# Eight Strassen pairs in each feed-forward layer, the first of them begun in the first token half

## The chip, the cores and the metric

The kernel runs on one core of a Trainium2 chip. The metric is the time of one execution on the device in microseconds (us), less is better. Two kernels are compared by the median of several runs on the same chip.

## The reference

Two layers over one sequence of 512 tokens with 1024 channels. Layer 0 mixes the tokens with a causal multi-scale pooling, layer 1 with a causal differential attention; a SwiGLU feed-forward part follows each. All is fp32.

```python
D_MODEL, SEQ, DEPTH = 1024, 512, 2
D_FF = 2816

def _swiglu(x, w_gate, w_up, w_down):
    return (jax.nn.silu(x @ w_gate) * (x @ w_up)) @ w_down

def reference(x, ...):
    for i in range(DEPTH):
        h = _multiscale_pool(...) if i % 2 == 0 else _diff_attention(...)
        x = _layernorm(ALPHA * x + h, ln_mix_g[i], ln_mix_b[i])
        x = _layernorm(ALPHA * x + _swiglu(x, w_gate[i], w_up[i], w_down[i]), ln_ffn_g[i], ln_ffn_b[i])
    return x
```

## The kernel before

**Numbers in two halves.** Each fp32 factor is split into a high and a low part of a shorter type. A product is three matmuls, high by high, high by low and low by high. A weight chunk of 512 KB comes from HBM into a tile `raw` (five of them), ACT casts its high part (`h`), and DVE subtracts to get the low part (`l`). Six pairs of weight tiles exist; a cast into one of them must wait until the product that last used it has ended. The tokens lie transposed in `xt`, in two halves of 256.

**Gate and up.** The 2816 hidden features are 22 blocks of 128, each with a gate and an up product. They are computed in three ways, in this order:
- *Early features*: while the mixer's last token blocks (2 and 3) are still being normalised and transposed, only the first token half exists. Layer 0 takes three features, layer 1 two, at 256 tokens, and then the same features once more for the second half. The dictionary `late` says after which product of the first half PE transposes block 2 or 3.
- *Plain features*: full width, 512 tokens, 48 matmuls of 512 for gate and up.
- *Strassen pairs*, `strassen(k)`: two features by two token halves make a 2x2 block product, done with seven half-size products of 24 matmuls of 256 instead of eight. The order on PE is `GATE = ("P1", "Q5", "P6", "Q3", "P7", "P2", "Q4")`. P1, P6, P7 and Q4 accumulate in the PSUM bank A, Q5 and Q3 in C, P2 in B. After a product the bank's content is read, by ACT or DVE, before the next product in that bank adds to it. Before, pairs 4 to 10 are done this way, seven in each layer.

P1 and P2 multiply token half 0 by plain weight chunks. The other products need sums: sums of weight chunks, which DVE adds in the raw tiles (line 636), and sums of the tokens' quarters, which DVE and ACT make once per layer (`sums_of_x`, lines 690 to 714, with their low parts in `xs`, line 696). DVE also makes the gated product `hid` (line 677), the layer norm's affine pair on the residual (227, 228), the sums of the down weights' terms (750, 751) and the sums of finished hidden rows (`sum_hidden`, 776 to 783). In a pair DVE subtracts Q3 (line 921) and P7 (line 923) from their banks.

**What sets the order.** The program is scheduled by hand: each engine executes its instructions in the order in which the code issues them. `advance` and `ahead` issue the steps that ready weight chunks, six chunks ahead of PE, in the order of the list `steps`. `ready` does that for the first chunks of a layer, `fetch` issues the loads on SP. `catch_up` issues one step of each open generator in `behind`. In the head of layer 0, `summed(s, ...)` (lines 183 and 190) adds the mixer's output to the residual of token block s and takes its statistics, `spread_of` ends them with a power on POOL (199), and `norm` (208) scales.

Of the kernel before, what the change touches and what calls it, by code (L numbers as in the profile page):

```python
# [12 lines left out]
F32 = mybir.dt.float32  # L13
# [3 lines left out]
ALU = mybir.AluOpType  # L17
# [37 lines left out]
def trunk(ctx, tc, x, wall, pscale, lam_p, subln, table, lng, lnb, band, first, onehot, out):  # L55
# [6 lines left out]
    def bank(name):  # L62
        return ps.tile([P, 512], F32, tag="bank", name=name)
# [19 lines left out]
    def load_x(s):  # L83
# [8 lines left out]
    divided = [0]  # L92
    total = wall.shape[0]
# [8 lines left out]
    rows_of_wall = list(range(total))  # L102
    rows_of_wall[attn : attn + 24] = order_of_rows
    added = {attn + 6 + r: vrow[1] + r for r in range(2)}
# [206 lines left out]
    with tc.tile_pool(name="pool", bufs=1) as pp:  # L311
# [221 lines left out]
    def ffn(layer, late):  # L533
        n = 2 * layer + 1
        final = n == 2 * DEPTH - 1
        c0 = base[0]
        c1 = c0 + 2 * FB
        tt = nc.vector.tensor_tensor
        with tc.tile_pool(name=f"ffn{layer}", bufs=1) as fp:
# [12 lines left out]
            def block(i, b):  # L552

                if PAIRS[i][1] == 2:
                    return wall[c1 + 4 * i + b]
                return wall[c1 + 20 + b // 2][:, (b % 2) * 512 : (b % 2 + 1) * 512]

# [31 lines left out]

            chunks, index, steps = [], {}, []  # L590

# [5 lines left out]

            for k in range(HALF):
                j0 = index[k] = len(chunks)
                c = c0 + 4 * k  # L600
                if k in SPLIT:

                    chunks += [(c, ()), (c, (c, c + 1)), (c, (c, c + 2)), (c + 2, ())]
                    chunks += [(c + 1, (c + 1, c + 2)), (c + 3, ()), (c, (c, c + 3))]
                    step("cast", j0)
                    for w in (
                        "low 0, sum 1, cast 1, sum 4, cast 3, cast 4, low 1, sum 2, cast 2, low 3, "
                        "low 2, sum 6, cast 5, cast 6, low 4, low 5, low 6"
                    ).split(", "):
                        steps.append((w[:-2], j0 + int(w[-1])))  # L610
                else:
                    for i in range(4):
                        chunks.append((c + i, ()))
                        step("cast", j0 + i)
                        step("low", j0 + i)
            uses = {}
# [114 lines left out]
            def load_terms(k):  # L731
                if k < HALF - 1:
                    c = c1 + 4 * (k // 2)
                    src = wall[c : c + 4][:, :, term_slice(k)].rearrange("(j r) p t -> p j r t", j=2)
                else:
                    src = wall[c1 + 20 : c1 + 22].rearrange("j p (r t) -> p j r t", r=2)
# [33 lines left out]
            def sum_hidden(k):  # L770
# [3 lines left out]
                u = fp.tile([P, 2, 256], F32, tag="u", name=f"u{layer}_{k}", bufs=1)  # L774
                v = fp.tile([P, 2, 2, 256], F32R, tag="v", name=f"v{layer}_{k}", bufs=2)
                tt(u[:, 0, :], first, second, op=ALU.subtract)
# [54 lines left out]
            sums = sums_of_x()  # L831
            ks = [range(4 * b, 4 * b + 4) for b in range(2)]
            by_part = [(0, 0, range(KB)), (0, 1, range(KB)), (1, 0, range(KB))]
            by_half = [(0, 0, ks[0]), (1, 0, ks[0]), (0, 0, ks[1]), (1, 0, ks[1])]
            by_half += [(0, 1, ks[1]), (0, 1, ks[0])]
            for lo in (0, 256):
                for f in range(early):
                    for i in range(2):
                        product(
                            accs[f][i], 2 * f + i, lo, lo + 256,  # L840
                            None if layer or lo else by_part if f or i else by_half,
                        )
                        if not lo and (f, i) in late:
                            late[f, i]()
                        if not lo:
                            advance(2 * early, True)
                    if lo:
                        advance(2 * f + 6)
# [3 lines left out]
                        if f < 2:  # L852
                            weight_sums()
                            next(sums)
                        if f == 1:
                            behind.append(sum_hidden(0))

            def plain(f):
                k = f // 2
                j = index[k] + 2 * (f % 2)  # L860
                a = (bank(f"g{layer}_{f}"), bank(f"u{layer}_{f}"))
# [7 lines left out]
                if f < SB:  # L869
                    affine(n - 1, f)  # L870
                if f in (3, 5, 7):
                    weight_sums()
# [5 lines left out]
            def strassen(k):  # L878
                names = {"P1": "A", "P6": "A", "P7": "A", "Q4": "A", "Q5": "C", "Q3": "C", "P2": "B"}
                banks = {b: bank(f"{b}{layer}_{k}") for b in "ACB"}  # L880
                lefts = {
                    "P1": [quarter(0, i, 0) for i in range(2)],
                    "P2": [quarter(0, i, 1) for i in range(2)],
                    "Q4": [quarter(1, i, 1) for i in range(2)],
                }
                for m, p in enumerate(("Q5", "P6", "P7", "Q3")):
                    lefts[p] = [xs[:, m, i] for i in range(2)]
# [3 lines left out]
                def both(t):  # L891
                    return t.rearrange("p (f t) -> p f t", f=2)
# [4 lines left out]
                for j, p in enumerate(GATE):  # L897
                    acc = banks[names[p]]
                    h, l = halves[index[k] + j]
                    xh, xl = lefts[p]  # L900
                    for f in range(2):
                        o = acc[:, f * 256 : (f + 1) * 256]
                        for kk in range(4):
                            c = slice((4 * f + kk) * P, (4 * f + kk + 1) * P)
                            for e, (w, x) in enumerate(((h, xh), (h, xl), (l, xh))):
                                nc.tensor.matmul(  # L906
                                    o, w[:, c], x[:, kk, :],
                                    start=p in ("P1", "Q5", "P2") and f + kk + e == 0,
                                    stop=p in ("Q4", "Q3", "P2") and (f, kk, e) == (1, 3, 2),
                                    skip_group_check=True,  # L910
                                )
                    acc = both(acc)
# [16 lines left out]
                    ahead(index[k] + j + 6)  # L929
                    catch_up()  # L930
# [116 lines left out]
    def attention():  # L1047
        n = 2
        with tc.tile_pool(name="attn", bufs=1) as ap:
# [420 lines left out]

    ffn(0, {(1, 0): later(0, 2), (1, 1): later(0, 3)})
    attention()
# [109 lines left out]
```

## Time and profile before

| | |
|---|---|
| median of three runs | 939.98 us (939.54 to 940.16) |
| the profiled execution | 940.01 us, span 938.2 us |
| mean granted clock of PE | 0.998 |
| PE busy | 925.0 us, 99% |
| DVE busy | 789.8 us, 84% |
| ACT busy | 512.9 us, 55% |
| POOL busy | 126.7 us, 14% |
| mean DMA rate | 225 GB/s |

The time of an execution is 1.8 us longer than the span from the first to the last instruction. PE's share of the span leaves 13.2 us in which it had no matmul. A row of a timeline gives start, duration, engine, line, operation, output and inputs, the shape, the count, and in brackets the idle time ahead of it with what ended that. Lines are those of the kernel before.

### The profile page before, as it was taken

To read this page: it belongs to the slowest core of one execution; us is meant where nothing else is said; L and a number is where in the kernel's file an instruction comes from. 1 tells how busy PE (TensorE), PEld (TensorE's weight loads), DVE (VectorE), ACT (ScalarE), POOL (GpSimd) and SP (SyncE) were. 2 spreads that over 40 slices of the span, in tenths; PEclk is the share of its full clock that TensorE was granted. 3 is DMA by queue.
4 is the path that set the end of the run, shared out by engine and by line. 5 is a ranking of instruction groups with operands and counts; after the bars stand their busy time and mean duration, and the time that the engine had idled before them with its cause. 6 is when DMAs were issued, how large, how long until landed. Compare 5 with 4: busy or idle time off the path is not lost.

```text
span 938.2 us, 14939 instructions
## 1 busy us (share of the span) xinstructions
PE 925.0 (99%) x5710; PEld 827.2 (88%) x5710; DVE 789.8 (84%) x1166; ACT 512.9 (55%) x814; POOL 126.7 (14%) x152
## 2 busy tenths in 40 slices
PE   9999999999999999999999999999999999999996
PEld 8998899999988888888888887988899999988884
DVE  8969889999988778968888877788789999987678
ACT  6652444555564457667878754734245554654450
POOL 4221121110101201201112100211111110001101
PEclk9999999999999999999999999999999999999999
DMA  8487988886868988975666522597887885878942
GB/s 243 154 266 225 336 283 245 259 258 211 259 199 277 363 256 232 226 198 154 164 137 178 159 68 68 148 322 226 258 255 243 266 277 192 264 244 286 353 156 91
DMA packets 86038, 211.11 MB, mean 225 GB/s; under 512 B 15140, under 2 KB 26660, under 8 KB 85966
## 3 DMA queue, kind: packets, MB, share of 16 engines
q1 hardware_dynamic: 43420, 117.16, 38.1%
q0 software_dynamic: 18768, 58.20, 24.8%
q10 hardware_dynamic: 23778, 34.78, 10.4%
q8 instruction: 45, 0.74, 0.3%
q14 instruction: 27, 0.22, 0.1%
HBM read 173.40 MB, written 36.72 MB: 224 GB/s over the span
## 4 chain that ended last, share of the span: by engine, by line
PE 92%; DVE 5%; ACT 1%; issue 1%; DMA 0%; POOL 0%; DVEq 0%; ACTq 0%; POOLq 0%
PE A L906 17%; PE P L973 14%; PE C L906 9%; PE Q L973 6%; PE B L906 4%; PE g L150 3%; PE u L150 3%; PE g L149 3%; PE u L151 3%; PE u L149 3%; PE g L151 3%; PE s L1192 2%; PE va L1123 2%; PE wo L150 1%; PE wo L151 1%; PE q L149 1%
## 5 line engine op out<-in xcount | busy, mean ns | idle before, releaser
L636 DVE TENSOR_TENSOR raw<-raw,raw 128x1024 f32<-128x1024 f32 x56 | 68.3, 1219 | 0.5
L123 ACT CAST xs<-hid 128x512 fp32r<-128x512 f32 (+1 forms) x60 | 34.7, 581 | 24.4 <-DVE hid L813 24.4
L124 DVE TENSOR_TENSOR xs<-hid,xs 128x512 fp32r<-128x512 f32 (+1 forms) x60 | 38.5, 643 | 7.8 <-ACT xs L123 7.8
L1212 ACT ACTIVATE p<-p,mn 128x128 f32<-128x128 f32 (+3 forms) x64 | 35.2, 552 | 14.1 <-DVE mn L1207 14.1
L249 ACT ACTIVATE y<-pt,bT,gT 128x128 f32<-128x128 f32 x72 | 27.1, 456 | 26.6 <-PE pt L235 23.5
L744 POOL DMA_DIRECT2D b<-in_wall x20 | 14.0, 706 | 172.4 <-DMA tsum<-b 68.8
L805 POOL DMA_DIRECT2D xs<-ssum x24 | 17.4, 725 | 140.8 <-PE Q L973 67.8
L677 DVE TENSOR_TENSOR hid<-sg,u 128x512 f32<-128x512 f32 x16 | 11.0, 687 | 25.5 <-PE u L151 14.7
L199 POOL TENSOR_TENSOR rs<-rs,mhalf 128x1 f32<-128x1 f32 x16 | 12.8, 800 | 140.9 <-DVE rs L198 97.3
L744 POOL DMA_DIRECT2D hid<-in_wall x24 | 18.9, 831 | 77.5 <-DMA tsum<-hid 50.2
L1207 DVE CUSTOM_DVE_ANT_0 p<-s,bias 128x128 f32<-128x128 f32 (+3 forms) x64 | 28.0, 485 | 1.1 <-PE s L1192 1.1
L781 ACT CAST v<-u 128x512 fp32r<-128x512 f32 x22 | 13.7, 621 | 26.9 <-DVE u L779 26.8
L190 DVE BATCH_NORM_STATS2 st<-res 128x6 f32<-128x512 f32 x32 | 22.2, 694 | 1.1
L932 ACT ACTIVATE sg<-sg 128x512 f32<-128x512 f32 x14 | 8.9, 633 | 26.0 <-DVE sg L925 26.0
L745 POOL DMA_DIRECT2D hid<-in_wall x12 | 14.8, 1233 | 55.1 <-DMA hid<-in_wall 55.1
L693 ACT CAST xs<-hid 128x1024 fp32r<-128x1024 f32 x8 | 8.4, 1051 | 24.0 <-DVE hid L710 11.6
L124 DVE TENSOR_TENSOR xt<-y,xt 128x512 fp32r<-128x512 f32 x18 | 12.3, 691 | 10.9 <-ACT xt L123 10.7
L921 DVE TENSOR_TENSOR hid<-C,hid 128x512 f32<-128x512 f32 x14 | 9.7, 691 | 10.7 <-PE C L906 9.2
L1226 DVE SCALAR_TENSOR_TENSOR p<-p,sm,p 128x128 f32<-128x128 f32 (+3 forms) x32 | 17.6, 551 | 1.1
L917 ACT COPY hid<-C 128x512 f32<-128x512 f32 x14 | 8.2, 588 | 18.2 <-PE C L906 18.2
L124 POOL TENSOR_TENSOR sql<-sq,sqh 128x512 fp32r<-128x512 f32 x7 | 9.3, 1324 | 60.5 <-ACT sqh L123 60.5
L745 POOL DMA_DIRECT2D b<-in_wall x10 | 12.3, 1230 | 38.0 <-DMA b<-in_wall 38.0
(1211 smaller groups left out, 3637.1 us busy)
## 6 DMA issues: line engine op xcount, KB each, us to landing
raw<-in_wall SPq DMA_DIRECT2D x122, 512.0 KB, 5.0
r<-tsum SPq DMA_DIRECT2D x40, 512.0 KB, 4.5
hid<-in_wall POOLq DMA_DIRECT2D x36, 512.0 KB, 7.3
b<-in_wall POOLq DMA_DIRECT2D x30, 512.0 KB, 5.8
r<-in_wall SPq DMA_DIRECT2D x30, 512.0 KB, 4.5
tsum<-hid ACTq DMA_DIRECT2D x24, 512.0 KB, 5.4
ssum<-v ACTq DMA_DIRECT2D x22, 512.0 KB, 3.8
tsum<-b ACTq DMA_DIRECT2D x20, 512.0 KB, 4.9
```

The costliest lines, as they stand in the source:

```text
L123: nc.scalar.copy(dst_h, src)
L124: (low or nc.vector).tensor_tensor(dst_l, src, dst_h.bitcast(F32), op=ALU.subtract)
L149: nc.tensor.matmul(acc, ah, bh, start=start, stop=False)
L150: nc.tensor.matmul(acc, ah, bl, start=False, stop=False)
L151: nc.tensor.matmul(acc, al, bh, start=False, stop=stop)
L249: nc.scalar.activation(y[:, k, :], pt[:, k * P : (k + 1) * P], AF.Identity, bias=bT[:, n, kk : kk + 1], scale=gT[:, n, kk : kk + 1],)
L636: tt(t, raws[pair[0]], raws[pair[1]], op=ALU.add)
L744: nc.gpsimd.dma_start(out=t[:, j], in_=src[:, j])
L906: nc.tensor.matmul(o, w[:, c], x[:, kk, :], start=p in ("P1", "Q5", "P2") and f + kk + e == 0, stop=p in ("Q4", "Q3", "P2") and (f, kk, e) ...
L973: nc.tensor.matmul(accs[s], x[:, k, r], y[:, c], start=first and k == 0 and e == 0, stop=last and k == m - 1 and e == 2, skip_group_check= ...
L1207: nc.vector.tensor_tensor_reduce(out=p, in0=accs[c], in1=biases[h][:, w - 1 :: -1] if w < S else biases[h][:, ::-1], op0=ALU.add, op1=ALU. ...
L1212: nc.scalar.activation(p, p, AF.Exp, bias=mn[:, q, c : c + 1], scale=-1.0, accum_out=sm[:, q, c : c + 1],)
```

## The change

The number of Strassen pairs goes from seven to eight in each layer: pair 3 is a pair now. Layer 0 has two early features instead of three and four plain ones instead of five, layer 1 one instead of two and five instead of six. In the place of the early feature that went, the first token half has P1 and P2 of pair 3, whose two weight chunks are fetched there, and fetched again when pair 3's other products come (four more loads of 512 KB in all). Their sum waits in a tile `g3` of its own. `strassen(3)` skips P1 and P2.

Other edits come with it. In layer 0 the transposes of token block 3 stand behind P1 instead of behind the up product of feature 1. The weight chunk of that up product (`w5`) is made ready ahead of `summed(3)`. The first product of the second token half goes by half of the channels. The tile `v` has one buffer instead of two. The first two steps of `sums_of_x` come in the first half. At the end of the attention the second of two scalings comes behind `ready` instead of ahead of it. DVE has 1169 rows instead of 1149, PE 4433 instead of 4472 (a row may stand for several instructions), SP 240 instead of 236.

```diff
-SPLIT = (4, 5, 6, 7, 8, 9, 10)
+SPLIT = (3, 4, 5, 6, 7, 8, 9, 10)
+EARLY = (2, 1)
...
+    def rows_of_ffn(layer, c):
+        g = list(range(c, c + 2 * FB))
+        e, pair = 2 * EARLY[layer], c + 4 * SPLIT[0]
+        return g[:e] + [pair, pair + 3] + g[e:] + list(range(c + 2 * FB, c + 3 * FB))
...
         norm(0, 2)
+        ready(6)
         summed(3, 0, 1)
         spread_of(0, 3)
-        ready(6)
         norm(0, 3)
...
+            for f in range(2 * SPLIT[0]):
+                for i in range(2):
+                    plain_chunk((f, i), row(2 * f + i))
+                if f == early - 1:
+                    plain_chunk((SPLIT[0], 0, "pair"), c0 + 2 * early)
+                    plain_chunk((SPLIT[0], 5, "pair"), c0 + 2 * early + 1)
+            for k in SPLIT:
...
+                if k > SPLIT[0]:
+                    step("cast", number[k, 0, "pair"])
+                for w in (
+                    "low 0, sum 1, cast 1, sum 4, cast 3, cast 4, low 1, sum 2, cast 2, low 3, "
+                    "low 2, sum 6, cast 5, cast 6, low 4, low 5, low 6"
+                ).split(", "):
+                    if k > SPLIT[0] or w[-1] not in "05":
+                        steps.append((w[:-2], number[k, int(w[-1]), "pair"]))
...
-                v = fp.tile([P, 2, 2, 256], F32R, tag="v", name=f"v{layer}_{k}", bufs=2)
+                v = fp.tile([P, 2, 2, 256], F32R, tag="v", name=f"v{layer}_{k}", bufs=1)
...
-            early = 3 if layer == 0 else 2
...
+            halved = [(w, e, ks[b]) for b in range(2) for w, e in ((0, 0), (1, 0), (0, 1))]
+            g3 = fp.tile([P, S], F32, name=f"g3_{layer}")
+            ready_first = 2 * early + 2
             for lo in (0, 256):
                 for f in range(early):
...
+                if not lo:
+                    bankA, bankB = bank(f"A{layer}_{SPLIT[0]}"), bank(f"B{layer}")
+                    half_product(bankA, number[SPLIT[0], 0, "pair"], lefts["P1"], True, False)
+                    if "P1" in late:
+                        late["P1"]()
+                    nc.scalar.copy(both(g3), both(bankA))
+                    next(sums)
+                    half_product(bankB, number[SPLIT[0], 5, "pair"], lefts["P2"], True, True)
+                    tt(both(g3), both(bankB), both(g3), op=ALU.add)
+                    next(sums)
...
+                begun = k == SPLIT[0]
+                banks = {"A": bankA if begun else bank(f"A{layer}_{k}"), "C": bank(f"C{layer}_{k}")}
+                banks["B"] = None if begun else bank(f"B{layer}_{k}")
...
+                for m, p in enumerate(GATE):
+                    if begun and p in ("P1", "P2"):
+                        if p == "P2":
+                            g0 = g3
+                            nc.scalar.activation(g0, g0, AF.Silu)
+                        continue
                     acc = banks[names[p]]
...
-                if s in (0, 3):
-                    scaled(last - 1 if s == 0 else last)
+                if s == 0:
+                    scaled(last - 1)
                 ready(cw + min(5 + s, WBUFS) if s < 3 else cw + 8)
+                if s == 3:
+                    scaled(last)
...
-    ffn(0, {(1, 0): later(0, 2), (1, 1): later(0, 3)})
+    ffn(0, {(1, 0): later(0, 2), "P1": later(0, 3)})
```

**The first pair of layer 0.** Names: `A0_3` is bank A of layer 0, pair 3; `g0_17h` and `g0_17l` are the high and low part of weight chunk 17 of that layer; `xs` holds the sums of tokens, `xt` the tokens. PE before, in pair 4, from the end of P7 (chunk 20) over P2 (chunk 21) to the start of Q4 (chunk 22):

```order
L906 MATMUL A0_4_1338<-xs0_532,g0_20h_1265 128x256 x2
L906 MATMUL A0_4_1338<-xs0_532,g0_20l_1266 128x256
...
L906 MATMUL B0_4_1340<-xt_63,g0_21h_1368 128x256 x2
L906 MATMUL B0_4_1340<-xt_63,g0_21l_1369 128x256
...
L906 MATMUL A0_4_1338<-xt_63,g0_22h_1371 128x256 x2
L906 MATMUL A0_4_1338<-xt_63,g0_22l_1372 128x256
```

And now, in pair 3, from the end of Q3 (bank C, chunk 16) over P7 (chunk 17) to the start of Q4 (chunk 18):

```order
L867 MATMUL C0_3_1211<-xs0_532,g0_16h_1085 128x256 x2
L867 MATMUL C0_3_1211<-xs0_532,g0_16l_1086 128x256
L867 MATMUL A0_3_678<-xs0_532,g0_17h_1088 128x256 x2
L867 MATMUL A0_3_678<-xs0_532,g0_17l_1089 128x256
...
L867 MATMUL A0_3_678<-xt_63,g0_18h_1200 128x256 x2
L867 MATMUL A0_3_678<-xt_63,g0_18l_1201 128x256
```

P2 in bank B no longer stands between P7 and Q4; both use bank A.

DVE at the same place, before, with Q3's subtraction (line 921) and P7's (923) in pair 4:

```order
L642 TENSOR_TENSOR g0_22l_1372<-raw18_1063,g0_22h_1371 128x1024
L642 TENSOR_TENSOR g0_23l_1417<-raw22_1218,g0_23h_1416 128x1024
L783 TENSOR_TENSOR v0_3_1384<-u0_3_1383,v0_3_1384 128x2x256
L921 TENSOR_TENSOR hid0_531<-C0_4_1339,hid0_531 128x2x256
L636 TENSOR_TENSOR raw22_1218<-raw22_1218,raw23_1304 128x1024
L636 TENSOR_TENSOR raw23_1304<-raw23_1304,raw24_1375 128x1024
L642 TENSOR_TENSOR g0_24l_1477<-raw22_1218,g0_24h_1476 128x1024
L923 TENSOR_TENSOR hid0_531<-hid0_531,A0_4_1338 128x2x256
```

And now, in pair 3, with Q3's subtraction (line 972) and P7's (974); 660 is the raw sum, 666 the low part, 807 the low part of `v`:

```order
L666 TENSOR_TENSOR g0_20l_1285<-raw20_1078,g0_20h_1284 128x1024
L972 TENSOR_TENSOR hid0_531<-C0_3_1211,hid0_531 128x2x256
L660 TENSOR_TENSOR raw20_1078<-raw20_1078,raw22_1198 128x1024
L666 TENSOR_TENSOR g0_22l_1289<-raw22_1198,g0_22h_1288 128x1024
L666 TENSOR_TENSOR g0_21l_1323<-raw20_1078,g0_21h_1322 128x1024
L807 TENSOR_TENSOR v0_2_1253<-u0_2_1252,v0_2_1253 128x2x256
L974 TENSOR_TENSOR hid0_531<-hid0_531,A0_3_678 128x2x256
```

Between the two subtractions there were two raw sums and one low part; now there are one raw sum, two low parts (of the chunks 22 and 21) and the low part of `v`. The order in layer 1 is the same, with chunks of that layer.

**The head of layer 0.** DVE before, from the norm of token block 2 to the low part of chunk 4 (`mix3` is the mixer's output for block 3):

```order
L208 TENSOR_SCALAR res_67<-res_67,mv0_2_492,rs0_2_494 128x1024
L183 SCALAR_TENSOR_TENSOR res_67<-res_67,mix3_0_400 128x512
L190 BN_STATS st0_3_505<-res_67 128x6
L183 SCALAR_TENSOR_TENSOR res_67<-res_67,mix3_1_401 128x512
L190 BN_STATS st0_3_505<-res_67 128x6
L196 BN_AGGR mv0_3_509<-st0_3_505 128x2
L198 TENSOR_SCALAR rs0_3_511<-mv0_3_509 128x1
L124 TENSOR_TENSOR w5l_517<-raw5_328,w5h_516 128x1024
L208 TENSOR_SCALAR res_67<-res_67,mv0_3_509,rs0_3_511 128x1024
L642 TENSOR_TENSOR g0_4l_574<-raw6_330,g0_4h_573 128x1024
```

And now:

```order
L217 TENSOR_SCALAR res_67<-res_67,mv0_2_492,rs0_2_494 128x1024
L133 TENSOR_TENSOR w5l_507<-raw5_328,w5h_506 128x1024
L192 SCALAR_TENSOR_TENSOR res_67<-res_67,mix3_0_400 128x512
L199 BN_STATS st0_3_511<-res_67 128x6
L192 SCALAR_TENSOR_TENSOR res_67<-res_67,mix3_1_401 128x512
L199 BN_STATS st0_3_511<-res_67 128x6
L205 BN_AGGR mv0_3_515<-st0_3_511 128x2
L207 TENSOR_SCALAR rs0_3_517<-mv0_3_515 128x1
L217 TENSOR_SCALAR res_67<-res_67,mv0_3_515,rs0_3_517 128x1024
L666 TENSOR_TENSOR g0_4l_573<-raw6_330,g0_4h_572 128x1024
```

The low part of `w5` went from behind the statistics of block 3 to ahead of its residual. On PE, the up product of feature 1 (`w5`) was followed by the transposes of block 3 (`pt0_3`):

```order
L659 MATMUL u0_1_538<-xt_63,w5h_516 128x256 x16
L659 MATMUL u0_1_538<-xt_63,w5l_517 128x256 x8
L235 MATMUL pt0_3_0_679<-ident_68,res_67 128x128 x4
L235 MATMUL pt0_3_1_680<-ident_68,res_67 128x128 x4
L659 MATMUL g0_2_539<-xt_63,g0_4h_573 128x256 x16
L659 MATMUL g0_2_539<-xt_63,g0_4l_574 128x256 x8
```

Now P1 of pair 3 (bank A, with chunk 4) stands between, and P2 (bank `B0`, with chunk 5) comes after the transposes:

```order
L683 MATMUL u0_1_538<-xt_63,w5h_506 128x256 x16
L683 MATMUL u0_1_538<-xt_63,w5l_507 128x256 x8
L867 MATMUL A0_3_678<-xt_63,g0_4h_572 128x256 x2
L867 MATMUL A0_3_678<-xt_63,g0_4l_573 128x256
...
L244 MATMUL pt0_3_0_704<-ident_68,res_67 128x128 x4
L244 MATMUL pt0_3_1_705<-ident_68,res_67 128x128 x4
L867 MATMUL B0_679<-xt_63,g0_5h_575 128x256 x2
L867 MATMUL B0_679<-xt_63,g0_5l_576 128x256
```

P1 needs the low part of chunk 4 from its third matmul on; the gate product of feature 2 before took all its 16 matmuls with the high part first.

More of the change, by code (lines that the diff above doesn't have):

```diff
@@ L536, in ffn @@
         c0 = base[0]
-        c1 = c0 + 2 * FB
+        c1 = c0 + 2 * FB + 2
+        down = rows_of_wall[c0] + 2 * FB
+        early = EARLY[layer]
         tt = nc.vector.tensor_tensor
@@ L585, in refill @@
                     held[0] += 1
-            chunks, index, steps = [], {}, []
+            chunks, number, steps = [], {}, []
             def step(kind, j):
@@ L596, in step, with plain_chunk @@
                     steps.append((kind, j))
[L598 to L615, printed above, removed]
+            def plain_chunk(key, c):
+                number[key] = len(chunks)
+                chunks.append((c, ()))
+                step("cast", number[key])
+                step("low", number[key])
@@ L831, in ffn, with both, half_product @@
             sums = sums_of_x()
+            def both(t):
+                return t.rearrange("p (f t) -> p f t", f=2)
+            def half_product(acc, j, left, start, stop):
+                h, l = halves[j]
+                xh, xl = left
+                for f in range(2):
+                    o = acc[:, f * 256 : (f + 1) * 256]
+                    for kk in range(4):
+                        c = slice((4 * f + kk) * P, (4 * f + kk + 1) * P)
+                        for e, (w, x) in enumerate(((h, xh), (h, xl), (l, xh))):
+                            nc.tensor.matmul(
+                                o, w[:, c], x[:, kk, :],
+                                start=start and f + kk + e == 0,
+                                stop=stop and (f, kk, e) == (1, 3, 2),
+                                skip_group_check=True,
+                            )
+            lefts = {
+                "P1": [quarter(0, i, 0) for i in range(2)],
+                "P2": [quarter(0, i, 1) for i in range(2)],
+                "Q4": [quarter(1, i, 1) for i in range(2)],
+            }
+            for m, p in enumerate(("Q5", "P6", "P7", "Q3")):
+                lefts[p] = [xs[:, m, i] for i in range(2)]
             ks = [range(4 * b, 4 * b + 4) for b in range(2)]
```

77 lines of the change are left out of this document (34 added, 43 removed).

## The prediction

> **What bounds the kernel now.** I read the page's busy times first, then PE's waits, then the chain of waits by time, and last the busy times of a stretch in which the first layer's Strassen pairs run.
>
> ```profile
> PE 925.0 (99%) x5710; PEld 827.2 (88%) x5710; DVE 789.8 (84%) x1166; ACT 512.9 (55%) x814; POOL 126.7 (14%) x152
> ```
> ```profile
> PE warm L355 <- POOL ident masks.py:199: 1.9, 1, 1.9
> PE u L659 <- DVE w5l L124: 0.8, 1, 0.8
> PE wo L150 <- DVE w98l L124: 0.7, 1, 0.7
> ```
> ```profile
> 46.27 2.87 PE g L659 x24
> 49.13 2.88 PE u L659 x24
> 69.29 0.23 PE g L149
> ...
> 80.20 0.23 PE g L149
> ```
> ```profile
> 129.47 2.88 PE A L906 x24
> 132.35 2.88 PE C L906 x24
> 135.23 2.88 PE A L906 x24
> 138.11 2.88 PE B L906 x24
> ```
> ```profile
> 123.72:264.83 141.11, 141.11 (x1177) 141.11 (x1177) 132.71 (x161) 72.88 (x93) 13.14 (x15) 1.00 0.82 252
> ```
>
> PE works for 925.0 of 938.2 us, and its waits are almost nothing: 0.8 us in layer 0's head, 0.7 at the end of the attention. So matmuls removed are time removed, but every wait put into PE's stream is time added in full. The last row is the warning: between 123.72 and 264.83 PE is busy without a gap, and DVE (the third pair of numbers) for 132.71 of 141.11 us, 94%. Work that DVE must end within one product of PE has little room.
>
> **The matmuls.** A product of 24 half-width matmuls takes 2.88 us, so a Strassen pair of seven takes 20.16, and an early feature of four (gate and up, two token halves) 11.52. A plain feature takes 80.20 − 69.29 = 10.91. In each layer a pair takes the place of one early and one plain feature: 20.16 − 11.52 − 10.91 = −2.27 us, for two layers **−4.5**. That P1 and P2 of the new pair stand earlier changes no matmul. The Trainium skill ("TensorE: Matmul & The Clock Gate", section "Back-to-back issue gap") gives an isolated spacing of N/2.4 + 2.5 ns. By it this term would be an estimated −5.0 us; here the trace has 120 and 228 ns for what it puts at 109 and 216, and decides.
>
> **The new neighbour of P7.** With P2 gone from its place, Q4 follows P7 directly, and both use the bank A. Q4 writes into A from its first matmul; so PE must wait until DVE has read P7 from A (the subtraction of line 923 before, 974 now). Before, P2 with its 2.88 us in bank B lay between. These are DVE's steps there:
>
> ```profile
> 135.34 0.69 DVE L921 TENSOR_TENSOR hid<-C,hid 128x512 f32<-128x512 f32 x1 [1.40 <-PE C L906]
> 135.95 2.47 DVE L636 TENSOR_TENSOR raw<-raw,raw 128x1024 f32<-128x1024 f32 x2
> 138.34 1.22 DVE L642 TENSOR_TENSOR g_24l<-raw,g_24h 128x1024 fp32r<-128x1024 f32 x1
> 139.48 0.68 DVE L923 TENSOR_TENSOR hid<-hid,A 128x512 f32<-128x512 f32 x1
> ```
>
> P7 ended at 138.11, its subtraction at 140.16, and Q4 began at 140.99: before, a lateness of 2.05 us was hidden by P2. Now nothing hides it. And in the new order more stands ahead of that subtraction: since Q3's subtraction a raw sum, the low parts of g_22 and g_21, and v. The low part of g_21 needs its cast on ACT, and the weight slot for that cast comes free only when P7 has ended. The least stall is therefore a cast, a low part, v and the subtraction:
>
> ```profile
> 35.88 1.05 ACT L639 CAST g_4h<-raw 128x1024 fp32r<-128x1024 f32 x1 [0.41 <-ACT line L517]
> ```
>
> 1.05 + 1.14 + 0.60 + 0.68 = 3.5 us. But DVE doesn't come on time. I price its row in steps from start to start, from the stretch before that has the same operations:
>
> ```profile
> 84.34 1.23 DVE L707 TENSOR_TENSOR hid<-hid 128x1024 f32<-128x1024 f32 x1
> 85.49 0.69 DVE L783 TENSOR_TENSOR v<-u,v 128x512 fp32r<-128x512 f32 x1
> 87.18 0.69 DVE L677 TENSOR_TENSOR hid<-sg,u 128x512 f32<-128x512 f32 x1 [1.01 <-ACT sg L676]
> 87.78 1.22 DVE L227 TENSOR_TENSOR res<-res,gb 128x1024 f32<-128x1024 f32 x1
> 89.04 1.23 DVE L228 TENSOR_TENSOR res<-res,gb 128x1024 f32<-128x1024 f32 x1
> 90.18 0.68 DVE L750 TENSOR_TENSOR hid<-hid 128x512 f32<-128x512 f32 x1
> 90.90 0.69 DVE L751 TENSOR_TENSOR hid<-hid 128x512 f32<-128x512 f32 x1
> 91.51 1.22 DVE L642 TENSOR_TENSOR g_12l<-raw,g_12h 128x1024 fp32r<-128x1024 f32 x1
> 92.64 1.22 DVE L710 TENSOR_TENSOR hid<-hid 128x1024 f32<-128x1024 f32 x1
> ...
> 94.91 0.42 DVE L776 TENSOR_TENSOR u<-hid 128x256 f32<-128x256 f32 x1
> ...
> 96.50 1.22 DVE L642 TENSOR_TENSOR g_13l<-raw,g_13h 128x1024 fp32r<-128x1024 f32 x1
> 97.64 1.22 DVE L714 TENSOR_TENSOR hid<-hid 128x1024 f32<-128x1024 f32 x1
> ...
> 100.99 0.69 DVE L677 TENSOR_TENSOR hid<-sg,u 128x512 f32<-128x512 f32 x1 [1.00 <-ACT sg L676]
> ```
>
> A 128x1024 step (low part, raw sum, sum of x) takes 1.14, one of 128x512 0.60, the affine pair 2.40, a pair of terms 1.33, the four small sums of the hidden rows 1.59 (94.91 to 96.50). From L707 to the next gated product pass 2.84 us, from L714 3.35, since the silu stands on ACT behind a cast that DVE feeds.
>
> Let T be the end of feature 2's up product, from which DVE has time to be level (its steps from feature 1's gated product up to there sum to 8.2 us, a plain feature takes 10.91). In the new DVE order then follow, in both layers alike:
> - gated 2, affine, a low part, two sums of x, v, a low part, the sum of line 729: 0.60 + 2.40 + 5 × 1.14 + 0.60 = 9.3, so line 731 (L707 before) begins at T + 9.4; gated 3 2.84 later, at T + 12.2.
> - gated 3, affine, terms, eight of 128x1024 and the four small sums: 0.60 + 2.40 + 1.33 + 9.12 + 1.59 = 15.0; line 738 (L714 before) at T + 27.3, gated 4 3.35 later, at T + 30.6.
> - from gated 4 to the end of P7's subtraction: twelve of 128x1024 (13.7), five of 128x512 (3.0), terms 1.33, small sums 1.59, and the subtraction's own 0.68, in all 20.3; end at **T + 50.9**.
>
> PE has three plain features and four products in that time: 32.73 + 11.52, so P7 ends at T + 44.25. The stall is 6.7 us, with the hand-off 6.8, twice: **+13.6**. Its lower bound is the 3.5 above. Its upper: a step that reads the result of the step ahead took 1.26 (87.78 to 89.04), and if half of the 25 steps do, 1.5 more, so 8.3.
>
> **The clock after the stall.** A stall this long is not in the trace of before, save at the ends. After the last matmul and at the start the rows show:
>
> ```profile
> 929.00:933.00 4.00, 0.19 (x1) 0.00 (x0) 3.90 (x9) 0.00 (x0) 0.92 (x1) 1.00 0.35 131
> 933.00:935.00 2.00, 0.00 (x0) 0.00 (x0) 1.31 (x2) 0.00 (x0) 0.00 (x0) 0.69 0.24 91
> 935.00:938.00 3.00, 0.00 (x0) 0.00 (x0) 0.00 (x0) 0.00 (x0) 0.00 (x0) 0.50 0.32 117
> ```
> ```profile
> 5.03 0.88 PE L404 MATMUL pool<-fh,xt 128*128 128x256 f32 x4 [0.19 <-ACT fh L123]
> 5.75 0.64 PE L404 MATMUL pool<-fl,xt 128*128 128x256 f32 x4
> ```
>
> PE's clock (the column behind POOL's) is still 1.00 in the first four microseconds of idleness and half from about 4.6 us on. At the start the matmuls before 5.75 came 0.18 us apart, those after it 0.12; PE had been at work since 1.9, so 3.8 us went slowly, about half of them lost. I take 2.0 us for each of the two stalls, **+4.0**; the bounds are 0 (the clock stays) and 3.8 each. The Trainium skill (same page, section "Part 1: The HAM clock gate") states a free-running window of about 3.4 us: half clock after an idle window, full again after a busy one. By it I would estimate 1.7 to 3.4 us for each stall; the trace's tail agrees with it, and a stall in mid-kernel no run here shows yet.
>
> **The head of layer 0.** w5l now goes ahead of block 3's residuals on DVE, P1 takes the place of feature 2's gate product, and block 3's transposes come behind P1.
>
> ```profile
> 42.58 1.23 DVE L124 TENSOR_TENSOR w5l<-raw,w5h 128x1024 fp32r<-128x1024 f32 x1
> 44.24 0.81 DVE L208 TENSOR_SCALAR res<-res,mv,rs 128x1024 f32<-128x1024 f32 x1 [0.44 <-POOL rs L199]
> ```
> ```profile
> 42.80 1.41 POOL L199 TENSOR_TENSOR rs<-rs,mhalf 128x1 f32<-128x1 f32 x1 [4.06 <-DMA gb<-in_lng]
> ```
> ```profile
> 577.51 0.57 POOL L199 TENSOR_TENSOR rs<-rs,mhalf 128x1 f32<-128x1 f32 x1 [31.93 <-DVE rs L198]
> ```
>
> The wait of 0.8 for w5l goes, and u of feature 1 ends at about 43.75. DVE's row for block 3 moves 1.14 back, so its rs ends near 43.7. POOL's power took 1.41 beside a big DVE step and 0.57 beside an idle DVE, which it now has; the norm follows at 44.55, the low part of g_4 from 45.3 to 46.5. P1's third matmul needs it: PE waits about 2.5 us. With the rest of P1 (2.6), the transposes (0.8) and P2 (2.88) the second half begins at 52.8, against 49.13 + 2.88 and a little, 51.85, before: **+1.0**, or +1.85 with the power at 1.41.
>
> **Small edits.** At the end of the attention the scaling that stood ahead of w98l now stands behind the weights: the 0.7 goes, part of it comes back at the next norm, **−0.6** (0 to −0.9). The four extra fetches of 512 KB are spread over rows where PE never waited for a transfer: 0; if one is late, it costs its landing, 5 us at most. v with one buffer is cast anew only after a pair of features (21.8 us at 10.91 each), which its store has for leaving: 0.
>
> **The sum**, against the profiled execution's 940.0 us (span 938.2; the median is 939.98): −4.5 + 13.6 + 4.0 + 1.0 − 0.6 = +13.5, so **953.5 us**.
>
> **Rivals.**
> - *The stall with no loss of clock*: 953.5 − 4.0 = 949.5. For it speaks that the trace has no stall in mid-kernel; against it the tail. Chance 0.2.
> - *DVE is level by Q3, and only the least stall of 3.5 is left*: under the 4.6 us at which the clock fell, so 940.0 − 4.5 + 7.0 + 1.0 − 0.6 = 942.9; anything between adds twice its part. For it: before, DVE waited 1.40 us for Q3. Against it: 10.91 us less PE time lie ahead of the first pair for the same sums. Chance 0.16.
> - *Not slower*: P7's subtraction runs as soon as P7 ends. Then each pair stalls for 0.8 us only, and 940.0 − 4.5 + 1.6 + 1.0 − 0.6 = 937.5. It decides if less than 2.05 us per layer is lost (half of 4.5 − 1.0 + 0.6). The low part of g_21 ahead in DVE's order, whose cast waits for P7, excludes it unless that order is not the one that runs. Chance 0.06.
> - *Deeper*: stalls of 8.3 us or a late transfer, 956 to 960. Chance 0.1.
> - *The forecast*, stalls of 6 to 7.5 us with the clock lost: 952 to 955.5, chance 0.48.
>
> **How the numbers follow.** The range from 945.0 to 957.5 holds the forecast, the case without clock loss, and the inner parts of the small and the deep case; about 2 in 10 lie outside. About 0.2% (1.9 us) can be told from no change. The not-slower case, a part of which ends within that bound, and the head's uncertainty give faster 0.05 and same 0.03; all the others are slower, 0.92.
>
> **What would show it.** Right: a PE wait of about 6.8 us on line 867 with bank A, released by DVE's line 974, once per layer; a granted clock below 1.00 right behind each; a wait of about 2.5 us for g_4l in the head; no wait for w5l or w98l. Wrong: line 974 starting within 1 us of P7's end, P7 and Q4 back to back, or PE waiting at another place, such as a raw row that lands late.

## The result: slower by 1.7%, and the profile after

The changed kernel takes 956.08 us (median of six runs, 955.09 to 957.14) against 940.07 us for the kernel before (six runs, 939.54 to 940.32). The ratio is 1.017, 95% interval 1.0157 to 1.0183. The forecast was 953.5 us in a range of 945.0 to 957.5, slower with a chance of 0.92. The profiled execution has a span of 953.4 us against 938.2.

The busy times of the page after come first, then all that PE waited for (in total, times, longest):

```profile
PE 925.9 (97%) x5758; PEld 831.9 (87%) x5758; DVE 808.9 (85%) x1186; ACT 521.5 (55%) x826; POOL 126.1 (13%) x152
```
```profile
PE A L867 <- DVE hid L974: 14.7, 2, 7.3
PE A L867 <- DVE g_4l L666: 2.3, 1, 2.3
PE warm L364 <- POOL ident masks.py:199: 1.9, 1, 1.9
PE pool L413 <- ACT fh L132: 0.3, 1, 0.3
PE pt L244 <- DVE res L217: 0.2, 1, 0.2
```

The first two rows are new and were forecast by name and place; the waits for w5l and w98l are gone. PE is no less busy than before although it has less to do, because some of its matmuls ran at half clock. The timeline of DVE after, in layer 0's first pair, shows the queue that makes the wait:

```profile
122.31 1.22 DVE L666 TENSOR_TENSOR g_20l<-raw,g_20h 128x1024 fp32r<-128x1024 f32 x1
123.44 0.68 DVE L972 TENSOR_TENSOR hid<-C,hid 128x512 f32<-128x512 f32 x1
124.04 1.21 DVE L660 TENSOR_TENSOR raw<-raw,raw 128x1024 f32<-128x1024 f32 x1
125.17 1.22 DVE L666 TENSOR_TENSOR g_22l<-raw,g_22h 128x1024 fp32r<-128x1024 f32 x1
126.42 1.23 DVE L666 TENSOR_TENSOR g_21l<-raw,g_21h 128x1024 fp32r<-128x1024 f32 x1
127.56 0.68 DVE L807 TENSOR_TENSOR v<-u,v 128x512 fp32r<-128x512 f32 x1
128.17 0.68 DVE L974 TENSOR_TENSOR hid<-hid,A 128x512 f32<-128x512 f32 x1
```

And PE's timeline after around it, P7's last matmul and Q4's first; the last row is from the head of layer 0:

```profile
121.30 0.28 PE L867 MATMUL A<-xs,g_17l 128*128 128x256 f32 x1
128.90 0.80 PE L867 MATMUL A<-xt,g_18h 128*128 128x256 f32 x2 [7.32 <-DVE hid L974]
...
46.84 0.54 PE L867 MATMUL A<-xt,g_4l 128*128 128x256 f32 x1 [2.29 <-DVE g_4l L666]
```

DVE has no gap from 122.31 on. Q3 had ended by 118.54, where P7's matmuls begin, but DVE subtracts it only at 123.44: it is 4.9 us late. Four more steps follow before P7's subtraction ends at 128.85. Layer 1 has the same wait, 7.33 us. Behind each wait the clock is half, and it is half behind the short wait in the head too. These are the busy times by stretch after (PE first, the granted clock behind POOL's numbers):

```profile
44.00:47.00 3.00, 0.71 (x6) 0.51 (x5) 2.27 (x4) 1.22 (x3) 2.15 (x3) 0.99 0.68 221
47.00:50.40 3.40, 3.40 (x17) 3.40 (x18) 2.13 (x3) 0.00 (x0) 0.73 (x1) 0.51 0.89 349
...
121.00:125.00 4.00, 0.58 (x5) 0.37 (x4) 3.97 (x5) 3.46 (x4) 0.00 (x0) 1.00 0.98 387
125.00:129.00 4.00, 0.10 (x1) 0.10 (x1) 3.97 (x6) 1.15 (x2) 1.47 (x2) 0.55 0.30 111
129.00:132.00 3.00, 3.00 (x14) 3.00 (x15) 2.72 (x3) 0.52 (x1) 0.00 (x0) 0.50 0.90 259
132.00:136.00 4.00, 4.00 (x35) 4.00 (x34) 1.79 (x3) 1.54 (x2) 1.23 (x1) 0.97 1.06 365
```

In layer 1 PE worked longer at half clock:

```profile
694.20:698.80 4.60, 4.54 (x21) 4.54 (x22) 2.88 (x4) 0.63 (x1) 0.55 (x1) 0.50 1.00 345
```

In the head 16 matmuls took 3.53 us at half clock, behind the stall of layer 0 15 took 3.37, behind that of layer 1 21 took 4.63. At the 0.12 us from start to start that they take elsewhere, these are losses of 1.6, 1.6 and 2.1 us. The account of the spans: matmuls −4.5, waits +14.7 + 2.3 − 0.8 − 0.7 = +15.5, clock +5.3, together +16.3 against a measured +15.2. Of the rest of −1.1, 0.9 lies at the very end: from the start of DVE's last steps (line 219 before, 228 now) to the end of the span it is 5.3 us before and 4.4 after. Another 0.3 lies in the attention, which begins 9.8 us later than before and reaches its output product 9.5 us later. Why these two stretches are shorter is open.

### The profile page after: what moved, and what is told of

The parts are those of the page before. It is cut to its first block, busy times and chain, and to the rows that moved or that the text cites. A ratio compares the mean times of both kernels' runs of the same rounds, so it can differ in the third digit from the quotient of the medians.

```text
span 953.4 us, 15077 instructions
## 1 busy us (share of the span) xinstructions
PE 925.9 (97%) x5758; PEld 831.9 (87%) x5758; DVE 808.9 (85%) x1186; ACT 521.5 (55%) x826; POOL 126.1 (13%) x152
## 4 chain that ended last, share of the span: by engine, by line
PE 79%; DVE 13%; issue 3%; ACT 2%; DMA 1%; POOL 0%; DVEq 0%; ACTq 0%; POOLq 0%
PE A L867 19%; PE P L1024 13%; PE C L867 8%; PE Q L1024 6%; PE B L867 5%; PE va L1174 2%; PE s L1243 2%; PE q L158 2%; PE q L160 2%; PE k L158 2%; PE k L160 2%; PE q L159 2%; PE k L159 2%; DVE raw L660 1%; PE vc L1174 1%
## 5 line engine op out<-in xcount | busy, mean ns | idle before, releaser
L660 DVE TENSOR_TENSOR raw<-raw,raw 128x1024 f32<-128x1024 f32 x64 | 78.0, 1219 | 0.5
L768 POOL DMA_DIRECT2D b<-in_wall x20 | 14.0, 706 | 186.4 <-DMA tsum<-b 105.0
L133 DVE TENSOR_TENSOR xt<-y,xt 128x512 fp32r<-128x512 f32 x18 | 12.2, 689 | 13.8 <-ACT xt L132 13.8
L867 PE MATMUL A<-xt,g_18h 128*128 128x256 f32 x32 | 9.4, 392 | 14.7 <-DVE hid L974 14.7
L867 PEld LDWEIGHTS A<-xt,g_18h 128*128 128x128 f32 x32 | 7.8, 298 | 15.1 <-DVE hid L974 15.1
L968 ACT COPY hid<-C 128x512 f32<-128x512 f32 x16 | 9.4, 586 | 20.6 <-PE C L867 20.6
L701 DVE TENSOR_TENSOR hid<-sg,u 128x512 f32<-128x512 f32 x12 | 8.2, 684 | 12.5 <-PE u L160 7.3
```

Source lines behind the costliest of these rows:

```text
L133: (low or nc.vector).tensor_tensor(dst_l, src, dst_h.bitcast(F32), op=ALU.subtract)
L660: tt(t, raws[pair[0]], raws[pair[1]], op=ALU.add)
L867: nc.tensor.matmul(o, w[:, c], x[:, kk, :], start=start and f + kk + e == 0, stop=stop and (f, kk, e) == (1, 3, 2), skip_group_check=True,)
```

## The experiments

The theory has two parts: DVE is late in the first pair, and without P2 between P7 and Q4 that lateness stands in PE's stream, where it costs the clock too. The rival mechanisms are the weight slot (a least stall of 3.5 us), the clock being harmless, and DVE's lateness alone doing the harm, with or without P2. Each kernel was timed against the kernel before on the same chip (940.06 to 940.45 us).

**e1: PE kept busy during the wait.** Ahead of Q4 in pair 3:

```diff
+                    if begun and p == "Q4":
+                        idle = bank(f"F{layer}")
+                        for i in range(56):
+                            nc.tensor.matmul(
+                                idle[:, :256], halves[j][0][:, :P], lefts[p][0][:, 0, :],
+                                start=True, stop=True, skip_group_check=True,
+                            )
```

> Between P7 and Q4 of pair 3 PE gets 56 matmuls of 256 columns into an unused bank, in both layers (6.7 us of work that nothing reads). PE is then busy through most of the wait for DVE, and the wait itself still ends with DVE's subtraction. If the clock after the stall costs time, it stays at 1.00 here and each layer gains the 1.7 us that 3.4 us at half speed lose: 956.1 - 3.4 = 952.7 us. If only the wait costs, the time stays at 956.1. If the wait were not DVE's, the 56 matmuls would add up to 13.4 us.

Measured: 951.66 us (951.30 to 952.12). PE's waits in e1:

```profile
PE A L867 <- DVE g_4l L666: 2.3, 1, 2.3
PE warm L364 <- POOL ident masks.py:199: 1.9, 1, 1.9
PE A L867 <- DVE hid L981: 1.2, 2, 0.6
```
```profile
120.00:130.00 10.00, 9.38 (x79) 9.18 (x78) 9.93 (x11) 5.14 (x6) 1.48 (x2) 1.00 0.72 260
```

The clock stays at 1.00 in the stretch of e1 that holds the wait. More work on PE made the kernel 4.4 us faster (3.7 in the spans), near the 3.4 expected. The loss of clock is real: 1.6 and 2.1 us by the matmuls of the trace after, 1.9 for each wait by the spans of e1 and 2.2 by its median.

**e2: P7's subtraction ahead in DVE's queue.** In pair 3 Q3's `ahead` and `catch_up` come behind P7's subtraction:

```diff
+                    if begun and p == "Q3":
+                        continue
+                    if begun and p == "P7":
+                        ahead(j + 5)
+                        catch_up()
                     ahead(j + 6)
                     catch_up()
```

> In pair 3 the weight steps and the hidden-row step that follow Q3's subtraction on DVE come behind P7's subtraction. If DVE's queue ahead of the subtraction makes the stall, P7's subtraction ends right after Q3's, at about 124.7 us in layer 0's time of after's trace, against P7's end at 121.6: two stalls of 3.2 us instead of 7.3 and 7.4, so 956.1 - 8.3 = 947.8 us if the clock still drops, 944.4 if it does not. If the least stall of 3.5 us by the weight slot were what counts, or DVE were not the cause, it stays above 951.

Measured: 946.58 us (944.51 to 947.43). DVE and PE's waits in e2:

```profile
123.33 0.68 DVE L972 TENSOR_TENSOR hid<-C,hid 128x512 f32<-128x512 f32 x1
123.93 0.68 DVE L974 TENSOR_TENSOR hid<-hid,A 128x512 f32<-128x512 f32 x1
```
```profile
PE A L867 <- DVE hid L974: 6.4, 2, 3.2
PE A L867 <- DVE g_4l L666: 2.3, 1, 2.3
```
```profile
686.00:691.00 5.00, 5.00 (x24) 5.00 (x25) 4.96 (x6) 1.48 (x2) 1.55 (x3) 0.50 0.58 169
```

Two waits of 3.2 us instead of 7.3, as expected, less than the 3.5 us that the slot would set. So four DVE steps (4.1 us) of each stall were the queue between the two subtractions, and 3.2 us were the lateness that DVE brought along. A wait of 3.2 us still dropped the clock: 0.53 in 126 to 129 us. In layer 1 (the last row) the same wait cost more: PE was back at work at 685.85 and ran at half clock until about 692. So what a wait costs in clock is not fixed by its length: over the four executions of e2 the mean granted clock went from 0.990 in the longest to 0.996 in the shortest.

**e3 and e6: another product between P7 and Q4.** Pair 3 runs P6, Q5, P7, Q3, Q4, so Q3 in bank C covers the subtraction; the weight steps mostly come behind it. e6 then moves one step, v's cast:

```diff
-                for m, p in enumerate(GATE):
+                turn_of = ("P1", "P6", "Q5", "P7", "Q3", "P2", "Q4") if begun else GATE
+                for p in turn_of:
+                    m = GATE.index(p)
...
-                    ahead(j + 6)
+                    if begun:
+                        q = number[k, 1, "pair"]
+                        ahead(q + {"P6": 6, "Q5": 6, "P7": 7, "Q3": 9, "Q4": 10}[p])
+                    else:
+                        ahead(j + 6)
                     catch_up()
```

And in e6 on top of it:

```diff
-                    catch_up()
+                    if not begun or p != "Q5":
+                        catch_up()
```

> In pair 3 the products run in the order P6, Q5, P7, Q3, Q4 and most weight steps come behind P7's subtraction, so that Q3 (2.88 us in another bank) lies between P7 and Q4. By the theory both stalls and their clock loss go: 956.1 - 14.7 - 3.4 = 938.0 us. The rival is that DVE is late by so much that the wait only moves, to Q4 or into the next pair: 941 to 946 us.

> e3 with one edit: v's cast in pair 3 is issued behind P7's subtraction, not behind Q5. In e3 ACT stood 6.8 us at that cast, for the store that empties the only v buffer, and the cast of g_20 stood behind it. If that is the cause of e3's wait of 5.2 us and of its clock loss, the time falls from 944.2 to 938 or 939; if it is DVE's lateness alone, it stays at 943 to 945.

Measured: e3 944.17 us (943.29 to 946.23), e6 941.90 us (941.22 to 945.84). The stalls behind P7's subtraction in pair 3 were gone, but in e3 PE had others, in pair 4; their row among PE's waits, and ACT's timeline in e3:

```profile
PE A L867 <- ACT sg L968: 5.2, 2, 3.9
```
```profile
116.90 0.59 ACT L970 COPY hid<-C 128x512 f32<-128x512 f32 x1 [1.58 <-PE C L867]
124.32 0.62 ACT L805 CAST v<-u 128x512 fp32r<-128x512 f32 x1 [6.83 <-DMA ssum<-v]
124.85 1.04 ACT L663 CAST g_20h<-raw 128x1024 fp32r<-128x1024 f32 x1
```

ACT stood 6.83 us at v's cast, for the transfer that empties the only buffer of `v` (it was issued at 112.38 and landed 11.87 us later), and the cast of g_20 stood behind it. In e6 that ACT row begins at 124.33 without any wait, and the wait on L968 shrinks to this row of e6's waits:

```profile
PE A L867 <- ACT sg L968: 2.3, 2, 1.1
```

So the single buffer can cost time, though it cost none in the changed kernel, where that cast came later in ACT's row. e6's median was 3 us higher than the 938 to 939 expected: a wait of 2.5 us of PE for another copy by ACT (line 972) was new in its trace. That copy stood behind v's cast of pair 4, which waited for the same kind of transfer:

```profile
138.92 0.62 ACT L805 CAST v<-u 128x512 fp32r<-128x512 f32 x1 [3.57 <-DMA ssum<-v]
139.44 0.58 ACT L972 COPY hid<-A 128x512 f32<-128x512 f32 x1
```

So e6 moved the wait at the single buffer into the next pair and did not remove it. No run gives these orders the second buffer back.

**e4: the head.** P1 takes all 16 matmuls with the high part of the weights first, then the eight with the low part:

```diff
-                    half_product(bankA, number[SPLIT[0], 0, "pair"], lefts["P1"], True, False)
+                    for e, (w, x) in enumerate(((h, xh), (h, xl), (l, xh))):
+                        for f in range(2):
+                            for kk in range(4):
+                                nc.tensor.matmul(
...
```

> P1 of the first half takes its 16 matmuls with the high part of the weights first, so the low part of g_4 is needed 1.9 us after P1's start instead of 0.24 us. The wait of 2.3 us shrinks to about 0.8. If this wait is what dropped the clock for the 3.4 us behind it, that loss of 1.7 us goes as well: 956.1 - 3.2 = 952.9 us. If the clock drops all the same, 954.6.

Measured: 953.12 us (952.46 to 953.43). The wait for g_4l is 0.6 us, with this row in e4's waits, and the clock records of its trace have no half clock in the head:

```profile
PE A L917 <- DVE g_4l L666: 0.6, 1, 0.6
```

3.0 us less, as expected where the wait is what dropped the clock.

**e5: e6 and e4 together, with one chunk less prepared behind Q4.**

> e3's order of products (P6, Q5, P7, Q3, Q4) with v's cast issued behind P7's subtraction instead of behind Q5, the weight steps behind Q4 one chunk shorter, and P1 of the head taken with its high parts first as in e4. If the single v buffer made e3's remaining wait, the two waits of 5.2 us in all go to at most 1 us and no clock is lost: 956.1 - 14.7 - 3.4 - 3.0 (e4's gain) = 935.0, at most 936.5 us, faster than before's 940. If the wait is DVE's whole lateness and only moves on, 938 to 941.

Measured: 939.60 us (twelve runs, 937.73 to 946.78), ratio to before 1.0006 (0.9988 to 1.0024): not told apart from before, and in the range that was expected if the lateness only moves on. The profiled execution was the fastest of the twelve, with a span of 935.9 us and these waits:

```profile
PE C L867 <- ACT hid L979: 1.6, 2, 0.9
PE A L867 <- ACT hid L981: 0.7, 1, 0.7
PE A L917 <- DVE g_4l L666: 0.6, 1, 0.6
PE A L867 <- DVE hid L985: 0.5, 1, 0.5
```

All four are small and lie, but for the head's, in the pair after the first. The 0.7 us of line 981 again have v's cast ahead of them on ACT, which stood 1.81 us for its transfer. Of twelve executions three took 944.8 to 946.8 us; what they waited for is open, since only one execution has a trace; v's single buffer is a candidate that no run tests.

**e7: eight whole pairs, nothing begun early.** The kernel before with one line changed, `SPLIT = (3, 4, 5, 6, 7, 8, 9, 10)`; P2 stays where it was.

> The kernel before with eight whole pairs in each layer and nothing moved: pair 3 takes the place of two plain features, P2 stays between P7 and Q4. PE has 2 x (21.82 - 20.16) = 3.3 us less work. If the missing P2 makes the stall, none is seen and the time is 936.7 us. If DVE's lateness alone is enough, it is late by more than P2's 2.88 us too, and waits of 1 to 5 us in each layer take the gain: 938 to 945.

Measured: 943.70 us (943.19 to 944.01), ratio 1.0037 (1.0024 to 1.005). PE's waits in e7:

```profile
PE A L906 <- ACT sg L915: 2.8, 1, 2.8
PE warm L355 <- POOL ident masks.py:199: 1.9, 1, 1.9
PE A L906 <- DVE hid L923: 0.9, 2, 0.5
```

The wait for P7's subtraction is there even with P2 as a cover, 0.5 us in each layer. And ACT's copy of P1 (line 915) came 2.8 us late in layer 0, since the silu ahead of it stood behind a transfer that waited for DVE's low part of v:

```profile
109.31 0.60 ACT L676 ACTIVATE sg<-g 128x512 f32<-128x512 f32 x1 [3.64 <-DVE v L783]
```

So both hold: with eight pairs DVE and ACT have so little room in the first pair that the gain of 3.3 us is lost even without the early part, and without P2 the whole lateness of P7's subtraction becomes a wait. P2's part in that is its own 2.88 us. In layer 0 of e7 the subtraction comes 3.3 us behind P7 (0.45 and P2), not 7.3, but ahead of it PE had lost 2.8 us and worked for 3.4 us at half clock, time in which DVE could catch up; e7 doesn't tell these apart.

**e8: the end of the attention alone.** The kernel before with the second `scaled` behind `ready`.

> The kernel before with one edit: at the end of the attention the second scaling comes behind the making of the weights. The wait of 0.7 us for the low part of w98 goes and part of it comes back: 0.6 us less than before, between 0 and 0.9. In the traces it may show as the wait alone.

Measured: 939.30 us (eleven runs, 938.75 to 940.59), ratio 0.9990 (0.9981 to 0.9999). The row for w98l is no longer among the waits. This is the only version that was faster than before by its interval, by about 0.9 us.

**e9 and e10: work moved out of the first pairs.** e9 is e5, e10 is e7 with e8's edit; in both, DVE's sums of hidden row 2 move to pair 5 and one pair of term sums to pair 7 (e9's edit):

```diff
-                if f % 2:
+                if f in (1, 3):
                     weight_sums()
                 if f == 3:
                     load_terms(3)
-                if f % 2:
+                if f in (1, 3):
                     behind.append(sum_hidden(k))
...
+                    if k == 5 and p == "Q3":
+                        behind.append(sum_hidden(2))
...
+                if k == 7:
+                    catch_up()
+                    weight_sums()
```

> e5 with less on DVE ahead of and in the first pair: the sums of hidden rows 2 (1.6 us and v's low part 0.6) come in pair 5 and one pair of term sums (1.33 us) in pair 7. Same work, other places. If what is left of e5's waits (2.8 us in its trace) and its spread (937.7 to 946.8) come from DVE's and ACT's lateness in the first pairs, 3.5 us less there removes most of it: median 935 to 937 with a spread of 2 us. If the spread comes from elsewhere, the median stays near 939.6.

> e7 (eight whole pairs, nothing begun early) with the same relief as e9 and e8's place of the scaling. If e7's waits (2.8 us for ACT's copy of P1, 1.4 at other places, and 1.7 of clock) come from DVE's lateness in the first pair, they go: 943.7 - 5.9 - 0.6 = 937.2 us. If the wait for P1's copy has another cause (a weight that arrives late), 940 to 943.

Measured: e9 939.95 us (938.89 to 945.78), e10 945.28 us (943.37 to 948.02). Neither gained. PE's timeline in e9 shows where the time went:

```profile
168.84 0.51 PE L867 MATMUL A<-xs,g_35h 128*128 128x256 f32 x2 [0.45 <-ACT sg L977]
...
210.08 0.50 PE L867 MATMUL A<-xs,g_49h 128*128 128x256 f32 x2 [0.60 <-ACT sg L977]
...
729.14 0.51 PE L867 MATMUL A<-xs,g_35h 128*128 128x256 f32 x2 [0.46 <-ACT sg L977]
770.37 0.50 PE L867 MATMUL A<-xs,g_49h 128*128 128x256 f32 x2 [0.60 <-ACT sg L977]
```

These are new waits, the same in both layers, behind the pairs that got the work, and e10 has them too. The pairs have almost no room left on DVE: in e9's stretch from 720 to 820 us it is busy for 96.23 of 100 us. e10 was expected at 937.2, or at 940 to 943, and missed both. Its largest wait, 2.77 us for ACT's copy of P1, is that of e7: the steps that were moved come behind it in DVE's row, so the move could not reach it. Another wait, 1.4 us for ACT's copy of line 917, was new.

**e11: one low part of each pair on POOL.** e5 with the low part of Q4's chunk made by POOL.

```diff
-                        tt(l, t, h.bitcast(F32), op=ALU.subtract)
+                        on_pool = j in [number[k, 6, "pair"] for k in SPLIT]
+                        low = nc.gpsimd.tensor_tensor if on_pool else tt
+                        low(l, t, h.bitcast(F32), op=ALU.subtract)
```

> e5 with one low part of each pair (chunk of Q4, the last of the seven) made by POOL instead of DVE: 1.14 us less on DVE for each of 16 pairs, a POOL subtraction of 2.65 us for each (estimated as twice the 1.33 us that 128x512 takes in before's trace). If DVE's lateness with eight pairs makes the rest of e5's waits (2.8 us) and its spread, they go: median 935 to 936, spread 2 us. If POOL's work slows DVE beside it, or the low part is late behind POOL's transfers, 939 to 945.

Measured: 979.15 us (975.25 to 989.32), ratio 1.0421 (1.0379 to 1.0464). POOL's and DVE's timelines in e11 at the same time:

```profile
145.82 1.23 POOL L771 DMA_DIRECT2D hid<-in_wall  x1 [3.60 <-DMA hid<-in_wall]
146.60 2.82 POOL L668 TENSOR_TENSOR g_25l<-raw,g_25h 128x1024 fp32r<-128x1024 f32 x1
```
```profile
146.31 4.21 DVE L668 TENSOR_TENSOR g_30l<-raw,g_30h 128x1024 fp32r<-128x1024 f32 x1
```

The DVE step took 4.21 us instead of 1.22, 2.99 more, about the whole of POOL's 2.82: the two do not run beside each other, so nothing was taken from DVE. It is busy for 830.9 us in e11 against 808.4 in e5, with 16 steps fewer. The Trainium skill ("SBUF — State Buffer", section "SBUF: two separate sides") says that a GpSimd operation and a DVE operation with two SBUF inputs hold a shared port pair in turn, for a whole instruction; the trace agrees in the length, though by its records the DVE step began 0.29 us ahead of POOL's. POOL's low part also stood behind a transfer that POOL issues and that waited 3.60 us. The time is far outside both expectations: PE waits 15.6 us for low parts from POOL, 12.5 for P7's subtractions and 5.0 for ACT's copies.

## Why the prediction was right, step by step

- **The matmuls**, −4.5: no row speaks against it. e7 has 3.3 us less by the same prices; it shows 4.2 us of new waits and a loss of clock behind one of them, and came out 3.3 us slower. So the term itself was not measured apart from the waits.
- **The stall at P7**, forecast 6.8 us twice, measured 7.32 and 7.33. T was at 77.27 in the trace after. Feature 2's gated product began 0.27 behind it (0.1 forecast), feature 3's at 12.5 (12.2), feature 4's at 31.1 (30.6), and P7's subtraction ended at 51.6 (50.9). DVE had been level at T, as the working needs: it waited 0.96 us for that up product. The error of 0.5 us is mostly five steps of about 1.26 us where I had 1.14. The lower bound of 3.5 us was a bound of that order alone: e2 had 3.2, because its new order let the subtraction go ahead of g_21.
- **The clock**, forecast 2.0 us for each stall, measured 1.6 and 2.1, which e1 bore out with 4.4 us by medians for both. The estimate by the Trainium skill ("TensorE: Matmul & The Clock Gate", section "Part 1: The HAM clock gate") was 1.7 to 3.4; the trace is at the lower end. What failed is the tail's 4.6 us as the length that a wait needs: the clock fell behind waits of 2.29 us (the head) and 3.2 us (e2), so the rival with the least stall of 3.5 us, priced without a loss of clock, was priced too low.
- **The head**, forecast +1.0, was the step that was mis-sized: the second half began at 54.84 instead of 51.85, +3.0. The wait itself was right (2.29 against 2.5 us). I had not given it a loss of clock, since the tail kept full clock for 4.6 us; it cost 1.6 us more, and the whole of layer 0 began 0.3 us later. In the profiled execution (955.17 us) the forecast is 1.7 us short: 2.0 from the head and 1.1 from the stalls, less 0.3 from the clock and about 1.1 from the attention and the end, which I had not forecast. So a part of the head's error was hidden by luck.
- **Small edits**: the place of the scaling, −0.6, measured as about −0.9 by the ratio of times alone (e8), at the edge of the bounds. The extra fetches caused no PE wait. The single buffer of v cost nothing here, but the reason I gave, 21.8 us between casts, was wrong: in the trace after two of them are 16.8 us apart (107.2 and 124.0), and in e3 ACT was ready for the second at 117.5, while the store landed at 124.25. e6 lost time at the same buffer.
- **The rivals**: no loss of clock was excluded by e1. The least stall was excluded by the trace after, where ACT's cast of g_21 begins at 125.34, 3.8 us behind P7's end, and waits for DVE's raw sum. Not slower was excluded by both.

## What to carry to other kernels

A product that stands between a bank's reader and that bank's next writer is a cover; before it is moved, add up the reader's queue from the last point where its engine was level, because the wait that appears is the whole lateness and not the one step. Taking work off the critical engine gained nothing here, where DVE had about 5% of room: e5, e6, e9, e10 and e11 moved the wait from DVE's subtraction to ACT's copies, to later pairs and to POOL, and none of them was clearly faster than before. A part of ACT's lateness in e3, e5 and e6 is the single buffer of v, so a buffer that is given up has to be priced for the new order too. A short stall of the tensor engine can cost more than its length, so filling it, or ordering matmuls so that the late operand comes last, is worth trying first.

## What was not expected of the hardware

- A wait of 2.29 us in the head dropped the clock to half for the next 3.4 us, while e6 kept full clock over a wait of 2.5 us. At the same place in the kernel e7 lost its clock behind a wait of 2.79 us and e10 kept it behind one of 2.77. The Trainium skill ("TensorE: Matmul & The Clock Gate", section "Part 1: The HAM clock gate") speaks of an idle window of about 3.4 us; here less was enough, and not every time.
- 56 matmuls whose result nobody reads made the kernel 4.4 us faster.
- Beside a POOL subtraction of 2.82 us a DVE step took 4.21 us instead of 1.22.
